# Seven products instead of eight for the values and gates of two retention heads in a four-layer decoder trunk

## Chip, cores and metric

One core of a Trainium2 chip. The metric is the device time of one execution in microseconds, the median of several runs. All numbers are in fp32; a matmul operand is split into two fp32r parts, so that a product takes three matmuls.

## What is computed

Four layers on 256 tokens with 1024 features. The mixer of layer i is number i mod 3: retention in layers 0 and 3, dilated attention in layer 1, a gated MLP in layer 2. Each is followed by a SwiGLU channel mixer and a gated embedding of the layer. The change is about retention's values v and gates g:

```python
proj = h @ w_in
q, k, v, g = jnp.split(proj, [H * dk, 2 * H * dk, 2 * H * dk + H * dv], axis=-1)   # H=4, dk=256, dv=512
...
scores = jnp.einsum('bnhk,bmhk->bhnm', qc, kc) * decay_mask[None]
inner = jnp.einsum('bhnm,bmhv->bnhv', scores, vc)
...
y = y * lax.rsqrt(jnp.mean(y * y, axis=-1, keepdims=True) + EPS)
return (jax.nn.silu(g) * y) @ w_out
```

## The kernel before

All work is issued in the order in which the Python code runs (`tc.manual_schedule`); each engine takes its own instructions strictly in that order. PE is TensorE, DVE is VectorE, ACT is ScalarE, SP issues all loads.

**Weights.** Every weight is streamed once, as a list of entries per layer (`_plan`), 128 x 1024 values each, two entries to a load of 1 MB into a ring of four `raw` buffers. `split_one` (line 197) makes of an entry a chunk that a matmul can read: ACT copies it to `wh` (line 204), DVE takes the rest to `wl` (line 208). `USES` lists the chunks in the order in which they are used; one entry can be used several times, and a use can first add another entry to it in place (line 207, an add on DVE). Splits are pumped ahead: each `Chunk(...)` in the code takes the next chunk and lets one more be split, at most `LEAD = 6` beyond the one taken. `pump(n)` and the table `P` place further splits at fixed points.

**Products.** `token_major` (line 367) multiplies 256 tokens with 512 columns: four chunks of 12 matmuls of 512 columns, 48 in all. `feature_major` (line 335) makes 256 columns for q, k and the like: two chunks of 24 matmuls of 256 columns. Results lie in the PSUM pool "ps" with four banks; `acc`, in four other banks, collects the output projection, `row` adds one row block of `w_out` (12 matmuls of 512 columns).

**Retention** (line 477) goes over four heads `hd`. For each: v by `token_major`, evacuated by `ev_v` (ACT to `vh`, DVE to `vl`); then `t_of(z)`, the transposes of the head before; q and k by `feature_major` and their rotation on DVE (`ta`, `tb`, `qkl`) and ACT (`qkh`); g by `token_major` (`ev_g`, ACT to `sg`), with the scores (`sc`, `sh`, `sl`) before its last chunk; two rows of `w_out` for the head before; the two products `ys`; their norm (squares `junk` and square root on ACT, reciprocal on DVE) and `z`; two more rows.

**The channel mixer** (line 962) already has two blocks, `seven(i)`, in which gate and up of 512 columns are made by seven half-size products (Strassen's scheme in Winograd's form) instead of eight: p1, p5, p6, p1 again with more, p7, p3, p4, each of two chunks with six matmuls of 512 columns. Its left operands are blocks of `a_hi`, `a_lo` and four sums of such blocks, `s0` to `s3`, which `make_sums` prepares once per layer: 13 operations of 512 columns on DVE (9 sums and 4 rests) and 4 copies on ACT. The right ones are weights added in place: a unit of 8 entries gives 14 chunks with 8 adds. The results are put together on DVE in `u2`, `u4` and `up1`. There p4 is added to p7 in p7's own bank, which DVE must have read before (line 1099, `hid`).

Of the kernel before, what the change touches and what calls it, by code (L numbers as in the profile page):

```python
# [31 lines left out]
    rate=1, s0=2, s1=1, i0=2, i1=1, ar0=0, ar1=0, ar2=1, a0=0, a1=1,  # L32
# [21 lines left out]
def _plan(l):  # L54
    kind, j = l % 3, l // 3
    emb = _rows("ple_w_proj", l, 0, 2)
    mix = []
    if kind == 0:
        for h in range(4):
            mix += _cols("ret_w_in", j, 2048 + 512 * h, 512, 2)  # L60
            mix += _blocks("ret_w_in", j, 256 * h, 2) + _blocks("ret_w_in", j, 1024 + 256 * h, 2)
            mix += _cols("ret_w_in", j, 4096 + 512 * h, 512, 2)
            if h:
                mix += _rows("ret_w_out", j, 4 * h - 4, 2)
                mix += emb if h == 3 else []
                mix += _rows("ret_w_out", j, 4 * h - 2, 2)
        mix += _rows("ret_w_out", j, 12, 4)
    elif kind == 1:
        for p in range(8):
            cols = tuple((g * 3072 + 2048 + 128 * p, 128) for g in range(3))  # L70
            mix += [("attn_w_in", j, 2 * c, 2, cols) for c in range(4)]
            for g in range(3):
                for w in range(2):
                    mix += _blocks("attn_w_in", j, g * 3072 + w * 1024 + 128 * p, 1)
        mix += emb + _rows("attn_w_out", j, 0, 8)
    else:
        for c0 in (2048, 2560, 3072, 3584, 0, 512, 1024):
            mix += _cols("gm_w_in", j, c0, 512, 2)
        mix += _rows("gm_w_out", j, 0, 4) + _cols("gm_w_in", j, 1536, 512, 2)
        mix += _rows("gm_w_out", j, 4, 6) + emb + _rows("gm_w_out", j, 10, 6)  # L80
    mix += _cols("ffn_w_in", l, 0, 512, 2) + _cols("ffn_w_in", l, HID, 512, 2)
    uses = [(e, None) for e in range(len(mix))]

    def plain(ds):
        uses.extend((len(mix) + i, None) for i in range(len(ds)))
        mix.extend(ds)

    for i, seven in UNITS:
        if seven:
# [1224 lines left out]
```

## Time and profile before

| | |
|---|---|
| runs | 1703.89, 1704.80, 1705.27 us; median 1704.8 us |
| profiled execution | 1703.74 us, span 1702.0 us (1.7 us lie around the span) |
| PE busy | 1685.1 us (99%), 9867 matmuls |
| DVE busy | 1309.8 us (77%), 1851 instructions |
| ACT busy | 1037.9 us (61%), 1578 instructions |
| loaded | 311 MB, 184 GB/s over the span |

Busy time is the union of an engine's rows. A matmul's row goes from its start to the modelled end of its results, and the next one starts before that; the distance of starts is its pace. "Idle before" and the waits name what an engine waited for last.

### The profile page before, as it was taken

The numbers are of one execution on the slowest core, as the hardware profiler recorded it, in microseconds if no ns is written. First come the engines' busy times: TensorE is split into PE (matmuls) and PEld (weight loads), VectorE is DVE, ScalarE is ACT, GpSimd is POOL, SyncE is SP. The second block draws the span as 40 slices with busy tenths as digits, with TensorE's granted clock in tenths as the row PEclk, the third lists the DMA queues.
The fourth block names the chain that finished last, engine by engine and source line by source line (L and its number), as shares of the span: only waits on it lengthen the run. The fifth ranks groups of instructions, "written<-read, shape, count | busy, mean of one in ns | idle before, by whom it ended". The sixth has DMA issues, their size and how long they took to land.

```text
span 1702.0 us, 24880 instructions
## 1 busy us (share of the span) xinstructions
PE 1685.1 (99%) x9867; PEld 1492.8 (88%) x9867; DVE 1309.8 (77%) x1851; ACT 1037.9 (61%) x1578; POOL 0.2 (0%) x4
## 2 busy tenths in 40 slices
PE   9999999999999999999999999999999999999998
PEld 7888889888999999889888888898888888889887
DVE  7666578897888888778987675778977665678986
ACT  6555665557776767655567654745567555665555
POOL 0000000000000000000000000000000000000000
PEclk9999999999999999999999999999999999999999
DMA  8644453664655555453564744554464554553560
GB/s 291 227 154 178 170 210 124 223 223 151 200 178 166 170 171 178 124 207 124 223 247 149 280 178 151 191 206 177 173 221 167 192 183 173 176 208 124 223 241 31
DMA packets 53588, 314.14 MB, mean 185 GB/s; under 512 B 5632, under 2 KB 13616, under 8 KB 19168
## 3 DMA queue, kind: packets, MB, share of 16 engines
q1 hardware_dynamic: 53472, 312.56, 51.4%
q8 instruction: 77, 1.26, 0.3%
q14 instruction: 39, 0.32, 0.1%
HBM read 311.41 MB, written 1.12 MB: 184 GB/s over the span
## 4 chain that ended last, share of the span: by engine, by line
PE 84%; DVE 8%; ACT 4%; DMA 2%; issue 2%; ACTq 0%; SPq 0%; DVEq 0%
PE ps L237 18%; PE ps L239 18%; PE ps L238 18%; PE acc L237 7%; PE acc L239 7%; PE acc L238 7%; DVE wl L208 4%; ACT wh L204 2%; PE ps L357 2%; PE ps L358 2%; PE ps L361 2%; DMA raw<-in_w_dram 2%; DVE raw L207 1%; PE acc L295 1%; PE ps L286 1%
## 5 line engine op out<-in xcount | busy, mean ns | idle before, releaser
L208 DVE TENSOR_TENSOR wl<-raw,wh 128x1024 fp32r<-128x1024 f32 x615 | 715.0, 1206 | 85.4 <-ACT wh L204 82.0
L204 ACT ACTIVATE wh<-raw 128x1024 fp32r<-128x1024 f32 x615 | 608.4, 1040 | 117.0 <-DMA raw<-in_w_dram 44.0
L237 PE MATMUL ps<-a_hi,wh 128*128 128x256 f32 x1280 | 365.6, 286 | 0.0
L239 PE MATMUL ps<-a_hi,wl 128*128 128x256 f32 x1280 | 362.5, 283 | 0.0
L238 PE MATMUL ps<-a_lo,wh 128*128 128x256 f32 x1280 | 362.5, 283 | 0.0
L237 PE MATMUL ps<-wh,a_hi 128*128 128x512 f32 (+2 forms) x728 | 278.8, 383 | 7.5 <-DVE hid L1099 6.0
L238 PE MATMUL ps<-wl,a_hi 128*128 128x512 f32 (+2 forms) x728 | 276.2, 379 | 0.0
L239 PE MATMUL ps<-wh,a_lo 128*128 128x512 f32 (+2 forms) x728 | 276.1, 379 | 0.1
L238 PEld LDWEIGHTS ps<-a_lo,wh 128*128 128x128 f32 x1280 | 245.8, 192 | 0.9
L237 PEld LDWEIGHTS ps<-a_hi,wh 128*128 128x128 f32 x1280 | 245.7, 192 | 0.9
L239 PEld LDWEIGHTS ps<-a_hi,wl 128*128 128x128 f32 x1280 | 245.7, 192 | 0.0
L237 PEld LDWEIGHTS ps<-wh,a_hi 128*128 128x128 f32 x728 | 137.2, 188 | 34.8 <-ACT wh L204 9.1
L239 PEld LDWEIGHTS ps<-wh,a_lo 128*128 128x128 f32 x728 | 137.0, 188 | 24.3 <-DVE a_lo L300 0.9
L238 PEld LDWEIGHTS ps<-wl,a_hi 128*128 128x128 f32 x728 | 137.1, 188 | 23.2 <-DVE wl L208 0.8
L297 ACT ACTIVATE a_hi<-acc,gc 128x128 fp32r<-128x128 f32 x192 | 52.2, 382 | 43.6 <-PE acc L295 43.4
L207 DVE TENSOR_TENSOR raw<-raw 128x1024 f32<-128x1024 f32 x64 | 78.1, 1221 | 0.8
L237 PE MATMUL acc<-wh,h 128*128 128x512 f32 x192 | 75.0, 390 | 0.0
L238 PE MATMUL acc<-wl,h 128*128 128x512 f32 x192 | 74.9, 390 | 0.0
L239 PE MATMUL acc<-wh,h 128*128 128x512 f32 x192 | 74.8, 389 | 0.0
L237 PE MATMUL acc<-wh,hh 128*128 128x512 f32 x160 | 62.7, 392 | 0.0
L238 PE MATMUL acc<-wl,hh 128*128 128x512 f32 x160 | 62.4, 390 | 0.0
L239 PE MATMUL acc<-wh,hl 128*128 128x512 f32 x160 | 62.3, 389 | 0.0
(258 smaller groups left out, 2472.7 us busy)
## 6 DMA issues: line engine op xcount, KB each, us to landing
raw<-in_w_dram SPq DMA_DIRECT2D x266, 1024.0 KB, 5.0
raw<-in_w_dram SPq DMA_DIRECT2D x16, 768.0 KB, 4.5
gain<-in_norm_g_dram SPq DMA_DIRECT2D x8, 512.0 KB, 6.2
bias<-vec SPq DMA_DIRECT2D x8, 384.0 KB, 7.3
emb<-vec SPq DMA_DIRECT2D x8, 384.0 KB, 8.9
ln<-in_gm_ln_dram SPq DMA_DIRECT2D x2, 1024.0 KB, 7.5
raw<-in_w_dram SPq DMA_DIRECT2D x3, 512.0 KB, 8.3
dec<-in_c_decay_dram SPq DMA_DIRECT2D x4, 384.0 KB, 5.5
```

Of the source, the lines that this page charges most:

```text
L204: act.activation(out=hi[:, 0:n], in_=raw, func=AF.Copy)
L207: dve.tensor_tensor(out=entry(c + 1), in0=entry(c + 1), in1=entry(c + 1, 3), op=ALU.add)
L208: dve.tensor_tensor(out=lo[:, 0:n], in0=raw, in1=hi[:, 0:n].bitcast(F32), op=ALU.subtract)
L237: pe.matmul(ps, lhsT=lh, rhs=rh, start=start, stop=False, skip_group_check=more)
L238: pe.matmul(ps, lhsT=lh, rhs=rl, start=False, stop=False, skip_group_check=more)
L239: pe.matmul(ps, lhsT=ll, rhs=rh, start=False, stop=stop, skip_group_check=more)
L286: pe.transpose(ps[:, cut(i, 128)], src[:, cut(i, 128)], ident)
L295: pe.transpose(ps[:, cut(i, 128)], src[:, cut(i, 128)], ident)
L297: act.activation(out=dst_hi[:, k0 + i, tok(tt)], in_=ps[:, cut(i, 128)], func=AF.Copy, scale=gain(k0 + i))
L357: pe.matmul(ps, lhsT=a, rhs=w.hi[:, k, :], start=kk == 0, stop=False)
L358: pe.matmul(ps, lhsT=a, rhs=w.lo[:, k, :], start=False, stop=False)
L361: pe.matmul(ps, lhsT=a_lo[:, kk, tok(tt)], rhs=w.hi[:, k, :], start=False, stop=kk == 7)
```

## The change

In heads 1 and 3 of both retention layers (`SEVEN_HEADS`), v and g, 512 columns each, are made together by seven products like gate and up of the channel mixer, ahead of q and k. The code for it is taken out of `ffn` and shared: `make_sums` and `product_of_seven`. The sums of layer input blocks are made at the end of head 0. The transposes `t_of(z)` move between p3 and p4. `ev_seven` takes v and g of both token halves; g comes with its sign turned and gets a negative scale (`minus_r`). Since g is no longer made after k, the scores follow the first row of `w_out`. In `product_of_seven` p4 has a bank of its own, and `u2` gets p7 by one more sum on DVE; that holds for the channel mixer too. The vectors of the relative bias (`rel_vectors`), prepared in layer 0's retention in heads 1 to 3, are prepared in layer 0's channel mixer, in units 2 to 4. At the end of layer 0 two splits fewer are pumped before the second half of attention's input is transposed (rate 0 instead of 2 for `g2`, one later instead of none), and `i0` is 1 instead of 2. The scratch for dynamic DMAs is set to 1024.

```diff
-    rate=1, s0=2, s1=1, i0=2, i1=1, ar0=0, ar1=0, ar2=1, a0=0, a1=1,
+    rate=1, s0=2, s1=1, i0=1, i1=1, ar0=0, ar1=0, ar2=1, a0=0, a1=1,
...
+    def seven(name, j, c0, c1):
+        e = len(mix)
+        a, b = _cols(name, j, c0, 512, 2), _cols(name, j, c1, 512, 2)
+        mix.extend(b[0:2] + a[0:2] + b[2:4] + a[2:4])
+        for at, add in ((2, None), (2, 0), (2, 4), (6, None), (0, 4), (4, None), (6, 2)):
+            uses.extend((e + at + c, None if add is None else e + add + c) for c in range(2))
...
+            if h in SEVEN_HEADS:
+                seven("ret_w_in", j, 2048 + 512 * h, 4096 + 512 * h)
+            else:
+                plain(_cols("ret_w_in", j, 2048 + 512 * h, 512, 2))
...
+SEVEN_HEADS = (1, 3)
...
+    def make_sums(pool, temps):
+        t21, t11, s1 = temps
...
+        def split(n, t):
+            parts = [pool.tile([128, 4, 128], F32R, name=f"s{n}{p}") for p in "hl"]
+            act.activation(out=parts[0], in_=k4(t), func=AF.Copy)
+            dve.tensor_tensor(out=parts[1], in0=k4(t), in1=parts[0].bitcast(F32), op=ALU.subtract)
+            return parts
...
+    def product_of_seven(name, sums, temps, evac, middle):
+        def prod(a, ps=None):
+            more = ps is not None
+            ps = ps if more else ps_tile()
+            for c in range(2):
+                w = Chunk(name)
+                for k in range(2):
+                    kk = 2 * c + k
+                    mm3(ps, a[0][:, kk, :], a[1][:, kk, :], w.hi[:, k, :], w.lo[:, k, :], not more and kk == 0,
+                        kk == 3, more)
+                w.release()
+            return ps
+        u2, u4, up = temps
+        p1 = prod(block(0, 0))
+        act.activation(out=u2, in_=p1, func=AF.Copy)
+        p5 = prod(sums[0])
+        p6 = prod(sums[1])
+        dve.tensor_tensor(out=u2, in0=p6, in1=u2, op=ALU.add)
+        dve.tensor_tensor(out=u4, in0=p5, in1=u2, op=ALU.add)
+        prod(block(0, 1), p1)
+        evac(0, 0, p1)
+        p7 = prod(sums[2])
+        dve.tensor_tensor(out=up, in0=p7, in1=u4, op=ALU.add)
+        dve.tensor_tensor(out=u2, in0=p7, in1=u2, op=ALU.add)
+        p3 = prod(sums[3])
+        dve.tensor_tensor(out=u4, in0=p3, in1=u4, op=ALU.add)
+        evac(0, 1, u4)
+        middle()
+        p4 = prod(block(1, 1))
+        dve.tensor_tensor(out=u2, in0=p4, in1=u2, op=ALU.add)
+        evac(1, 0, u2)
+        evac(1, 1, up)
...
+            def ev_seven(tt, second, src):
+                if second:
+                    act.activation(out=sg[:, tt, :], in_=src, func=AF.Silu, scale=minus_r[tt])
+                else:
+                    ev_v(tt, src)
+
+            if hd in SEVEN_HEADS:
+                turned_z = []
+                product_of_seven(name, sums, sevens(), ev_seven, lambda: turned_z.append(t_of(z)))
+            elif hd:
                 token_major(name, ev_v)
...
-            if l == 0 and hd == 1:
-                rel_part = rel_vectors(mp)
-            if l == 0 and hd > 1:
-                rel_part[hd - 2]()
-            token_major(name, ev_g, before={3: scores})
+            if hd not in SEVEN_HEADS:
+                token_major(name, ev_g, before={3: scores})
+            if hd == 0 and SEVEN_HEADS:
+                sums = make_sums(mp, sevens())
...
                     row(w, zz, k, acc, hd == 1 and k == 0, False)
                     w.release()
+                    if k == 0 and hd in SEVEN_HEADS:
+                        scores()
...
-            prod(p7, block(1, 1), False, True)
-            dve.tensor_tensor(out=u2, in0=p7, in1=u2, op=ALU.add)
...
+            product_of_seven(name, sums, flats(), evac, lambda: rows(i - 1, ks=(0,)))
...
         pump(P["g1"])
-        st["rate"] = P["g2"]
+        to_attention = (l + 1) % 3 == 1
+        st["rate"] = 0 if to_attention else P["g2"]
...
-            pump(P["g4"])
+            pump(1 if to_attention else P["g4"])
...
-    nc = _bacc.Bacc("TRN2", target_bir_lowering=False, num_devices=1)
+    nc = _bacc.Bacc("TRN2", target_bir_lowering=False, num_devices=1, dynamic_dma_scratch_size=1024)
```

What this makes of the order shows at three places. (In rows of the changed kernel, lines are those of its own file: 215 is the add of raw weights, 216 the split on DVE, 245 to 247 the three matmuls of a product.)

DVE at the end of head 0 in layer 0, from the scores on. Before:

```order
27 L546 TENSOR_TENSOR sc<-ps,dec 128x384
28 L548 TENSOR_TENSOR sl<-sc,sh 128x384
29 L208 TENSOR_TENSOR wl<-raw,wh 128x1024
30 L272 RECIPROCAL sm<-sm 128x2
31 L582 SCALAR_TENSOR_TENSOR z<-ps,sm,sg 128x512 x2
32 L208 TENSOR_TENSOR wl<-raw,wh 128x1024 x4
33 L498 SCALAR_TENSOR_TENSOR vl<-ps,sm,vh 128x512 x2
```

Now, from the last of the sums on:

```order
47 L440 TENSOR_TENSOR pn<-pn,st 128x512
48 L422 TENSOR_TENSOR s3l<-pn,s3h 128x512
49 L657 TENSOR_SCALAR minus_572<-sm 128x1
50 L657 TENSOR_SCALAR minus_574<-sm 128x1
51 L280 RECIPROCAL sm<-sm 128x2
52 L687 SCALAR_TENSOR_TENSOR z<-ps,sm,sg 128x512 x2
53 L216 TENSOR_TENSOR wl<-raw,wh 128x1024 x2
54 L215 TENSOR_TENSOR raw<-raw 128x1024
55 L216 TENSOR_TENSOR wl<-raw,wh 128x1024
56 L215 TENSOR_TENSOR raw<-raw 128x1024
57 L216 TENSOR_TENSOR wl<-raw,wh 128x1024 x3
58 L463 TENSOR_TENSOR st<-ps,st 128x512
```

The 13 operations of the sums stand between the scores and `z`, and behind `z` begin the splits of head 1's block with their adds (rows 54 and 56).

PE at the beginning of head 1 in layer 0, with buffer numbers and waits. Before, the first product of the values:

```order
242 L239 MATMUL ps_544<-vh_166,sl_450 128x512
243 L237 MATMUL ps_544<-vh_166,sh_449 128x512
244 L238 MATMUL ps_544<-vl_167,sh_449 128x512
245 L239 MATMUL ps_544<-vh_166,sl_450 128x512
246 L237 MATMUL ps_569<-wh_408,a_hi_83 128x512 [waits Activation_49]
247 L238 MATMUL ps_569<-wl_409,a_hi_83 128x512
248 L239 MATMUL ps_569<-wh_408,a_lo_84 128x512
```

Now, the end of p5 and the product p6 (`ps_651`):

```order
267 L245 MATMUL ps_628<-wh_487,s0h_546 128x512
268 L246 MATMUL ps_628<-wl_488,s0h_546 128x512
269 L247 MATMUL ps_628<-wh_487,s0l_547 128x512
270 L245 MATMUL ps_651<-wh_520,s1h_553 128x512 [waits DVE_49,Activation_49]
271 L246 MATMUL ps_651<-wl_521,s1h_553 128x512
272 L247 MATMUL ps_651<-wh_520,s1l_554 128x512
273 L245 MATMUL ps_651<-wh_520,s1h_553 128x512
274 L246 MATMUL ps_651<-wl_521,s1h_553 128x512
275 L247 MATMUL ps_651<-wh_520,s1l_554 128x512
276 L245 MATMUL ps_651<-wh_607,s1h_553 128x512 [waits Activation_49]
277 L246 MATMUL ps_651<-wl_608,s1h_553 128x512 [waits DVE_49]
278 L247 MATMUL ps_651<-wh_607,s1l_554 128x512
```

The first matmul of p6 waits for DVE, though the first half of its weights was split long before: its bank is one that `z` has to read. The first matmuls of its second chunk wait for that chunk's split.

DVE in head 1 of layer 0 from the splits ahead of k's rotation to the reading of the scores (`sc`). Before:

```order
41 L208 TENSOR_TENSOR wl<-raw,wh 128x1024 x2
42 L521 TENSOR_TENSOR ta<-ps,turned 128x512
43 L522 TENSOR_TENSOR tb<-ps,turned 128x512
44 L523 TENSOR_TENSOR ta<-ta,tb 128x256
45 L524 TENSOR_TENSOR ta<-ta,tb 128x256
46 L528 TENSOR_TENSOR qkl<-ta,qkh 128x512
47 L208 TENSOR_TENSOR wl<-raw,wh 128x1024 x3
48 L546 TENSOR_TENSOR sc<-ps,dec 128x384
49 L548 TENSOR_TENSOR sl<-sc,sh 128x384
50 L208 TENSOR_TENSOR wl<-raw,wh 128x1024 x3
```

Now:

```order
80 L216 TENSOR_TENSOR wl<-raw,wh 128x1024 x2
81 L626 TENSOR_TENSOR ta<-ps,turned 128x512
82 L627 TENSOR_TENSOR tb<-ps,turned 128x512
83 L628 TENSOR_TENSOR ta<-ta,tb 128x256
84 L629 TENSOR_TENSOR ta<-ta,tb 128x256
85 L633 TENSOR_TENSOR qkl<-ta,qkh 128x512
86 L216 TENSOR_TENSOR wl<-raw,wh 128x1024
87 L646 TENSOR_TENSOR sc<-ps,dec 128x384
88 L648 TENSOR_TENSOR sl<-sc,sh 128x384
89 L216 TENSOR_TENSOR wl<-raw,wh 128x1024
```

One split lies between k's rotation and the scores instead of three, since a row of `w_out` has taken the place of three chunks of g.

## Rows read from the trace of the kernel before

**Rows 1.** The page: busy time of PE, and PE's granted clock by slice.

```profile
PE 1685.1 (99%) x9867; PEld 1492.8 (88%) x9867; DVE 1309.8 (77%) x1851; ACT 1037.9 (61%) x1578; POOL 0.2 (0%) x4
...
PEclk9999999999999999999999999999999999999999
```

**Rows 2.** Windows: us; busy us (count) of PE, PEld, DVE, ACT, POOL; clock; DMA.

```profile
48.00:58.92 10.92, 10.92 (x49) 9.05 (x49) 6.44 (x8) 7.97 (x12) 0.00 (x0) 1.00 0.34 129
59.82:71.38 11.56, 11.56 (x99) 11.56 (x98) 8.80 (x12) 5.51 (x8) 0.00 (x0) 1.00 0.39 137
```

**Rows 3.** Waits of PE: line, releaser, us in total, times, longest.

```profile
PE ps L237 <- DVE hid L1099: 6.0, 8, 1.1
PE ps L1219 <- DVE warm L1214: 1.5, 1, 1.5
PE ps L357 <- ACT a_hi L297: 1.2, 1, 1.2
PE ps L237 <- DVE band L956: 0.9, 1, 0.9
PE ps L237 <- DVE tb L522: 0.6, 1, 0.6
```

**Rows 4.** Timeline of DVE, layer 0, head 0's end: start, us, operation, count.

```profile
39.53 0.69 DVE L528 TENSOR_TENSOR qkl<-ta,qkh 128x512 fp32r<-128x512 f32 x1 [0.70 <-ACT qkh L527]
40.48 3.50 DVE L208 TENSOR_TENSOR wl<-raw,wh 128x1024 fp32r<-128x1024 f32 x3 [0.26 <-ACT wh L204]
43.89 0.55 DVE L546 TENSOR_TENSOR sc<-ps,dec 128x384 f32<-128x384 f32 x1
45.03 0.56 DVE L548 TENSOR_TENSOR sl<-sc,sh 128x384 fp32r<-128x384 f32 x1 [0.59 <-ACT sh L547]
...
51.61 0.17 DVE L272 RECIPROCAL sm<-sm 128x2 f32<-128x2 f32 x1 [4.40 <-ACT sm L270]
51.81 1.41 DVE L582 SCALAR_TENSOR_TENSOR z<-ps,sm,sg 128x512 f32<-128x512 f32 x2
```

**Rows 5.** Timeline of DVE in a block of seven products, layer 0's mixer.

```profile
286.88 1.22 DVE L207 TENSOR_TENSOR raw<-raw 128x1024 f32<-128x1024 f32 x1
...
289.27 1.23 DVE L207 TENSOR_TENSOR raw<-raw 128x1024 f32<-128x1024 f32 x1
...
304.75 0.68 DVE L1090 TENSOR_TENSOR gr<-ps,gr 128x512 f32<-128x512 f32 x1
...
308.93 1.22 DVE L208 TENSOR_TENSOR wl<-raw,wh 128x1024 fp32r<-128x1024 f32 x1 [1.64 <-ACT wh L204]
...
314.76 0.68 DVE L1099 TENSOR_TENSOR hid<-ps,gr 128x512 f32<-128x512 f32 x1
```

**Rows 6.** Timeline of DVE: first and last of 13 sum operations, layer 0's mixer.

```profile
252.92 0.68 DVE L1042 TENSOR_TENSOR gr<-a_hi,a_lo 128x512 f32<-128x512 f32 x1
...
263.79 0.69 DVE L1047 TENSOR_TENSOR s3l<-pn,s3h 128x512 fp32r<-128x512 f32 x1 [0.70 <-ACT s3h L1046]
```

**Rows 7.** Timeline of ACT, layer 0, head 0's end.

```profile
48.55 1.28 ACT L555 ACT_TABLE_LOAD   x1
49.84 0.60 ACT L266 ACTIVATE junk<-ps 128x512 bf16<-128x512 f32 x1
```

**Rows 8.** Timeline of PE: first matmul of y, head 0, layers 0 and 3.

```profile
45.80 0.39 PE L237 MATMUL ps<-vh,sh 128*128 128x512 f32 x1
...
1324.47 0.39 PE L237 MATMUL ps<-vh,sh 128*128 128x512 f32 x1
```

**Rows 9.** Timeline of DVE, head 1, layer 0: k's rotation, first and last.

```profile
71.88 0.68 DVE L521 TENSOR_TENSOR ta<-ps,turned 128x512 f32<-128x512 f32 x1
...
74.66 0.69 DVE L528 TENSOR_TENSOR qkl<-ta,qkh 128x512 fp32r<-128x512 f32 x1 [0.70 <-ACT qkh L527]
```

**Rows 10.** Timeline of DVE, layer 3, head 0: end of k's rotation.

```profile
1316.55 0.69 DVE L528 TENSOR_TENSOR qkl<-ta,qkh 128x512 fp32r<-128x512 f32 x1 [0.70 <-ACT qkh L527]
```

**Rows 11.** Timeline of PE: first matmul of p1, layer 0's mixer.

```profile
295.52 0.39 PE L237 MATMUL ps<-wh,a_hi 128*128 128x512 f32 x1
```

More of the change, by code (lines that the diff above doesn't have):

```diff
@@ L389, in token_major, with block, k4, pn @@
             evac(tt, ps[tt])
+    def block(tt, half):
+        return [t[:, 4 * half:4 * half + 4, tok(tt)] for t in (a_hi, a_lo)]
+    def make_sums(pool, temps):
+        t21, t11, s1 = temps
+        def k4(t):
+            return t.rearrange("p (k t) -> p k t", k=4)
+        def pn():
+            return tmp_p.tile([128, 512], F32, tag="pn", name="pn")
+        def whole(t, tt, half):
+            hi, lo = block(tt, half)
+            dve.tensor_tensor(out=k4(t), in0=hi.bitcast(F32), in1=lo.bitcast(F32), op=ALU.add)
+            return t
+        def split(n, t):
[3 more added lines that the diff above has]
+            return parts
+        sums = []
+        whole(t21, 1, 0)
+        t22 = whole(pn(), 1, 1)
+        dve.tensor_tensor(out=s1, in0=t22, in1=t21, op=ALU.subtract)
+        sums.append(split(0, s1))
+        whole(t11, 0, 0)
+        s2 = pn()
+        dve.scalar_tensor_tensor(out=s2, in0=s1, scalar=-1.0, in1=t11, op0=ALU.mult, op1=ALU.subtract)
+        sums.append(split(1, s2))
+        s3 = pn()
+        dve.tensor_tensor(out=s3, in0=t11, in1=t21, op=ALU.subtract)
+        sums.append(split(2, s3))
+        t12 = whole(pn(), 0, 1)
+        dve.tensor_tensor(out=t12, in0=t11, in1=t12, op=ALU.subtract)
+        s4 = pn()
+        dve.tensor_tensor(out=s4, in0=t12, in1=s1, op=ALU.add)
+        sums.append(split(3, s4))
+        return sums
@@ L490, in t_of, with sevens @@
             return zz
+        def sevens():
+            return [mp.tile([128, 512], F32, tag="st", name="st", bufs=3) for _ in range(3)]
         for hd in range(4):
@@ L509, in retention @@
             else:
[L510 removed]
+                zz = turned_z[0] if hd in SEVEN_HEADS else t_of(z)
             qk = []
@@ L934, in rel_vectors @@
     def rel_vectors(rp):
-        room = emb.rearrange("p a b -> p (a b)")[0:32, :]
-        hot, rel = room[:, 0:1152].rearrange("p (g u) -> p g u", g=3), room[:, 1152:1200]
+        rel = rp.tile([32, 48], F32, name="rel")
+        hot = rp.tile([32, 3, 384], F32, name="hot")
         band = rp.tile([16, 3, 384], F32, name="band")
@@ L1029, in rows @@
                     c.release()
-        sums = [[fp.tile([128, 4, 128], F32R, name=f"s{n}{p}") for p in "hl"] for n in range(4)]
-        def block(tt, half):
-            return [t[:, 4 * half:4 * half + 4, tok(tt)] for t in (a_hi, a_lo)]
-        def k4(t):
-            return t.rearrange("p (k t) -> p k t", k=4)
-        def whole(t, tt, half):
-            hi, lo = block(tt, half)
-            dve.tensor_tensor(out=k4(t), in0=hi.bitcast(F32), in1=lo.bitcast(F32), op=ALU.add)
-            return t
@@ new lines, in flats, with evac @@
+        def flats():
+            return [flat("gr"), flat("gr"), flat("hid")]
+        def seven(i):
+            s = [fp.tile([128, 512], F32, tag="s0", name="s0", bufs=2) for _ in range(2)]
+            def evac(tt, second, src):
+                if second:
+                    dve.scalar_tensor_tensor(out=hid0[tt], in0=src, scalar=-1.0, in1=s[tt], op0=ALU.mult, op1=ALU.mult)
+                else:
+                    act.activation(out=s[tt], in_=src, func=AF.Silu, scale=r[tt])
+            product_of_seven(name, sums, flats(), evac, lambda: rows(i - 1, ks=(0,)))
@@ L1124, in ffn @@
                 gain = load_gain(l, 3)
+                if l == 0:
+                    rel_part = rel_vectors(fp)
+            if l == 0 and i in (3, 4):
+                rel_part[i - 3]()
             up = feature_major(name)
@@ L1127, in ffn @@
             if i == 2:
-                make_sums()
+                sums = make_sums(fp, flats())
             rows(i - 2, i == NPAIR - 1)
```

113 lines of the change are left out of this document (28 added, 85 removed).

## Prediction

> **What bounds the kernel now.** I read the page first, then the waits of TensorE, then stretches of the timelines. The page says that TensorE is busy for 99% of the span, and at 9 tenths or more of full clock in each of the 40 slices [rows 1]. That share alone misleads, because a matmul's row lasts longer than the time to the next start. So I took the pace from stretches: 48 matmuls of 512 columns fill 10.92 us, 0.228 us each, and 96 of 256 columns fill 11.56 us, 0.120 us each [rows 2] (each window also counts a matmul or more that began before it). TensorE's waits are tiny: eight of 6.0 us in sum, one of 1.5 at the start, and single ones of 1.2, 0.9 and 0.6 us [rows 3]. TensorE therefore runs from start to end with hardly a hole. A matmul that goes saves its full pace, and each new wait is added in full to the end. The question is only whether the work that the change puts on VectorE (DVE) stays under TensorE's work.
>
> Prices on DVE: a split is 1.15 us (three take 3.50, the last of them 1.2 [rows 4]), an add of raw weights with the split behind it 2.39 us (from one add's start at 286.88 to the next at 289.27 [rows 5]), an operation on 512 columns 0.65 us (0.68 with its end [rows 5]).
>
> **What the change takes away.** In each of heads 1 and 3 of both retention layers, 96 matmuls for values and gates become 84. Four heads times 12 times 0.228 us: **-10.9 us**. In the dense channel mixer the fourth product gets a bank of its own, so the eight waits for `hid` go: **-6.0 us** [rows 3]. The added `u2` sum of 0.65 us on DVE is covered there: until TensorE needs what follows, it has a row and a feature-major product to do, over 8 us. At attention's opening two splits leave ScalarE's queue ahead of `a_hi`: **-1.2 us** [rows 3]; the later ones lie beside q and k products. I keep 0 to -4 as bounds, since pair 0's and pair 1's splits move too. The bias vectors' work moves out of head 3 of layer 0, where it cost waits of 0.9 and 0.6 us: **-1.5 us** [rows 3]. Its six small matmuls stay, now among units whose blocks take 2.9 us of TensorE per split of 1.15. Its three loads and one store on SP's queue move with it; the loads behind the store serve splits that come later on DVE too, so I cost that at nothing (at most, one wait for raw weights of 1.6 us, as in the mixer's unit [rows 5]). The smaller scratch for dynamic DMAs only makes room in SBUF, and I cost it at nothing: nothing in the order is issued from that engine. Together **-19.6 us**.
>
> **Opening of head 1, layer 0.** DVE is done with k's rotation at 40.22 (39.53 + 0.69 [rows 4]). Now three add-and-split pairs stand there instead of three splits: 7.2 us, to 47.4. The scores' chain `sc`, `sh`, `sl` lasts 1.7 us: it begins as the three splits end (43.89) and ends at 45.59 [rows 4]. Now it ends at 49.1. One more pair: 51.5. Then come the sums. In the channel mixer they took from 252.92 to 263.79, where `s3h` is done and the last split starts, 10.8 us with a round trip to ScalarE for each sum [rows 6]: 62.3 here. ScalarE's queue holds a table load (1.28) and the sums of squares behind `s3h`; from the first of these to DVE's reciprocal are 1.77 us, and 0.9 more to the end of the first `z` [rows 4, 7]. So `z` of the first half comes at **66.3**, of the second at 67.0.
>
> What waits for it: the pool "ps" has four banks. The two `y`, p1 and p5 hold them, so p6 needs a bank of `y`, and that comes back when `z` has read it. Before, a whole product of 48 matmuls [rows 2] lay between, and the next tile to need that bank was the transpose of `z` itself. TensorE ends the gates at 45.80 [rows 8]; `y` (9 matmuls), p1 and p5 (24) take 7.5 us, to 53.3. Hole: **13.0 us**.
>
> **The rest of that head.** DVE starts with no lead. Until it has read p7 for the second time it has 4 pairs, 6 splits and 5 operations of 512 columns: 9.6 + 6.9 + 3.3 = 19.8, from 67.0 to 86.8. p4 needs p7's bank (p3 and the two transposes hold the other three). TensorE, from 66.3, needs four products of 2.73 and 0.9 for transposes, to 78.1. Hole: 8.7. q needs p3's bank, which DVE reads two splits later: 0.2. After q and k (11.6 us) TensorE is at 101.3.
>
> Then the scores. The gates' last part used to lie between k and them, now only one row of `w_out` does (12 matmuls, 2.7 us, to 104.0). DVE still has two transposes' splits, four weight splits and two sums to do before q's rotation, at 97.0; with that (3.5 us, [rows 9]) and two splits k's begins at 103.0, 2.8 us before kh and 3.5 before kl can be used [rows 9]: holes of 1.8 and 0.5. If DVE were on time, 0.9 would be left, the lower bound. Sum for this head: 13.0 + 8.9 + 2.3 = **+24.2 us**.
>
> **Head 1, layer 3.** One pair fewer stands ahead of the scores. From 1317.24 [rows 10]: 6.2 to 1323.4, scores 1325.1 (TensorE asks for `sl` at 1324.92), a pair 1327.5, then 10.8 + 1.28 + 1.77 + 0.9: `z` at 1342.3 and 1343.0, and p6's first weights one pair later, 1345.4. TensorE would be ready at 1324.47 + 7.5 = 1332.0 [rows 8]: 13.4. Then 5 pairs, 5 splits and 5 small operations: 21.0, to 1364.0, against 1357.2: 6.8. With 0.2 and 2.3: **+22.7 us**.
>
> **Heads 3.** No sums are made here, and two rows of `w_out` on either side of `y` give DVE time. But p1 starts when DVE has only the fourth of fourteen splits ready, since `p_lo`, `z` and four adds lie ahead of it. By the same addition `u2` is done with p7 22.7 us after p1's start, and TensorE is there after 17.3 us (six products, transposes): 5.4. The channel mixer shows the nearest row: `hid`, read from p7, ended at 315.44, 19.9 us after p1's start at 295.52 [rows 5, 11], with a full lead; with the second read 20.6, which leaves 3.3, the lower bound. I take 5.0, nearer the addition, because the order has that work ahead of p1. With 2.3 for the scores: **+7.3 us** each, 14.6 for both.
>
> **Sum.** 24.2 + 22.7 + 14.6 = 61.5 of holes, less 19.6: +41.9. The profiled execution took 1703.7 us (span 1702.0), 1.1 below the median of the runs; 1703.7 + 41.9 + 1.1 = 1746.7, forecast **1746 us**. Its own range is 1732 to 1756: down to it reach 3.3 and 0.9 for the smaller holes (4 x 1.4 + 2 x 1.7 = 9 us) and 5 us for attention's opening and for pairs that come closer together; up, a wait for raw weights in each of the four blocks, of which the mixer's unit shows one of 1.64 us [rows 5], and nothing gained at attention's opening.
>
> **Rivals.** (1) *Faster, 1685 us.* DVE's lag stays covered, and only the -19.6 remain. For it: the mixer's units do the same arithmetic, and there TensorE waits only for `hid`. Place and point: the first `z` would have to come at 53.3 in layer 0, so the sums would have to begin 13 us earlier on DVE, before k's rotation, or DVE would have to be idle there. Against: it works without a pause from 40.5 to the scores even now [rows 4]. Chance 0.08.
> (2) *Only the openings cost, about 1716 us.* DVE catches up by p4, so that 13.0 + 13.4 and four times 0.9 remain: +30.0 - 19.6 = +10.4. It would take DVE operations that overlap more than the rows do; the mixer's lag of 19.9 speaks against it. Chance 0.13.
> (3) *The clock, about 1758 us.* The trace shows full clock everywhere [rows 1], and after the start no pause of TensorE longer than 1.2 us [rows 3], so no row tells what a hole of 9 to 13 us does. In my sum a slower p6 and p1' would cost nothing, because DVE sets p4's start. If half of q's product after p4 ran at half rate, 24 matmuls would cost 0.120 us more each, 2.9 us in each of four heads: +11.6. The Trainium skill, in "TensorE: Matmul & The Clock Gate", section "HAM oscillation — how this bites in real kernels", says that idle gaps of the engine send its clock back to half rate and that the work after each starts slow; no run here shows it yet, and it would give the 1758. Chance 0.08.
> (4) The change is there and moves nothing that can be measured: holes and savings cancel within 3.4 us. About 0.2% is what a measurement of this kernel can tell from no change. Chance 0.03.
>
> **Numbers.** Main case 0.68, (2) 0.13, (3) 0.08, (1) 0.08, (4) 0.03. The range 1714 to 1756 holds the main case and (2) and leaves out (1), (3) and most of (4), 0.19. Faster 0.08, same 0.03, slower 0.89.
>
> **What would show it.** The waits of TensorE must list `ps` on `z` of DVE, once in each retention layer, near 10 us; `ps` on DVE's `st` in all four heads, 3 to 9 us; and `qkh`/`qkl` at the scores. DVE's busy time must rise by about 100 us (per head 6 splits and 8 adds at 1.15 and six small sums; twice 13 operations of sums; 8 for the mixer), TensorE's must fall by some 11 while its idle time grows by 50 to 60. I am wrong if p6 finds its bank free, that is, if the gap between p5 and p6 in layer 0 is under 5 us, or if p4 starts within 18 us of p1.

## The result, and the profile after

The changed kernel takes 1766.7 us (median of four runs, 1765.0 to 1769.0), the kernel before 1704.4: a ratio of 1.0366, interval 1.0350 to 1.0381. The forecast was 1746, its range ended at 1756. The sign was right and so was the kind of cause, but 20.7 us are missing from the sum. The profiled execution has a span of 1763.3 us where that of before had 1702.0.

The page of the changed kernel, busy time of the engines and PE's granted clock by slice, against [rows 1]:

```profile
PE 1697.2 (96%) x9819; PEld 1494.0 (85%) x9819; DVE 1410.4 (80%) x1969; ACT 1069.5 (61%) x1614; POOL 0.2 (0%) x4
...
PEclk9899899999999999999999999999999899999999
```

TensorE runs 48 matmuls fewer, as forecast, and yet its busy time has grown by 12 us, where the prediction had it fall by 11; its idle time has grown by 49 (50 to 60 were forecast). VectorE's (DVE) busy time has grown by 100.6, as forecast. Why TensorE's has grown shows in the second row: three slices (44 to 88, 176 to 220 and 1367 to 1411 us) no longer stand at 9 tenths of full clock. All three lie in the retention layers.

The waits of PE (line, releaser, us in total, times, longest), against [rows 3]:

```profile
PE ps L245 <- DVE z L687: 17.9, 2, 9.0
PE ps L245 <- DVE st L469: 12.2, 4, 3.2
PE ps L245 <- ACT qkh L632: 11.4, 4, 4.4
PE ps L246 <- DVE wl L216: 5.9, 7, 2.1
PE ps L245 <- ACT sh L647: 2.2, 1, 2.2
...
PE ps L788 <- ACT th L777: 1.6, 1, 1.6
...
PE ps L245 <- DVE band L1060: 0.8, 1, 0.8
```

The first three waits are the three forecast ones: `z` twice, once in each retention layer; `st` in all four heads; `qkh` at the four scores. Two more are new: `wl`, of which 3.3 us stand behind the wait for `z` in layer 3, and `sh`, on which `y` of head 0 in layer 0 waits. The eight waits for `hid` ahead of the fourth product and the one for `a_hi` at attention's opening are gone. The wait for `band` is still there, in the mixer now, and one for `th` (1.6 us) stands in attention's first pair, where before had none as long.

The opening of head 1 in layer 0, first on DVE, then on PE (start, us, line, operation, in brackets the idle time before it and what ended it):

```profile
55.76 0.69 DVE L422 TENSOR_TENSOR s1l<-pn,s1h 128x512 fp32r<-128x512 f32 x1 [0.70 <-ACT s1h L421]
...
57.74 0.69 DVE L422 TENSOR_TENSOR s2l<-pn,s2h 128x512 fp32r<-128x512 f32 x1 [0.69 <-ACT s2h L421]
...
61.19 0.69 DVE L422 TENSOR_TENSOR s3l<-pn,s3h 128x512 fp32r<-128x512 f32 x1 [0.69 <-ACT s3h L421]
...
64.23 0.17 DVE L280 RECIPROCAL sm<-sm 128x2 f32<-128x2 f32 x1 [2.23 <-ACT sm L278]
64.44 1.41 DVE L687 SCALAR_TENSOR_TENSOR z<-ps,sm,sg 128x512 f32<-128x512 f32 x2
```

```profile
55.99 0.40 PE L247 MATMUL ps<-wh,s0l 128*128 128x512 f32 x1
65.33 0.76 PE L245 MATMUL ps<-wh,s1h 128*128 128x512 f32 x1 [8.95 <-DVE z L687]
```

DVE works through the sums, with a pause of 0.7 us for ScalarE (ACT) at each, before it comes to `z`, as in [rows 6]. p5 ends, p6 waits for a bank of `y`, and it starts as the first `z` has been read: at 65.3 us, where the forecast had 66.3.

Windows of PE: that hole, the 5.1 us behind it, and the time around the later hole ahead of p4 in head 3 (columns: window, its length, busy us and count, granted clock, DMA share, GB/s):

```profile
55.99:65.33 9.34, 0.39 (x2) 0.72 0.00 0
65.33:70.47 5.14, 5.14 (x12) 0.51 0.00 0
...
190.20:197.00 6.80, 5.37 (x14) 0.53 0.89 326
```

In the hole the granted clock falls, and p6's 12 matmuls run at 0.51, the lower of the clock's two levels (1.2 GHz): 5.1 us instead of the 2.73 of a product at full clock. A fall of the clock is what rival (3) rested on, which the forecast had given a chance of 0.08. The Trainium skill says in "TensorE: Matmul & The Clock Gate", section "HAM oscillation — how this bites in real kernels", that the clock goes back to half rate in such idle gaps, and the trace agrees (0.72 in the hole, 0.51 behind it). What it costs here is another matter, and the experiments answer it.

Where p4, the scores and `y` start, against the forecast. For layer 3 the forecast's times are moved by the 28.9 us by which the program is later at the end of head 0's gates. "Scores to y" was 4.7 us in the forecast: 4.2 by the pace of 24 matmuls (12 of 256 and 12 of 512 columns), and the hole of 0.5 for the rest of k, which lies behind the first scores.

| | forecast | measured |
|---|---|---|
| head 1, layer 0: p6 / p4 | 66.3 / 86.8 | 65.3 / 85.2 |
| head 1, layer 3: p6 / p4 | 1374.3 / 1392.9 | 1371.2 (its second matmul 1374.0) / 1392.6 |
| heads 3: p1 to p4 | 22.3 | 21.7 and 23.1 |
| p4 to the scores, all four heads | 19.0 | 21.82 in each |
| scores to y, all four heads | 4.7 | 6.4, 6.1, 6.3, 4.8 |

The openings and p4 came where they were forecast, to 2 us or better. What failed stands in the last two rows: 11.3 us too little between p4 and the scores, 4.8 behind them. The number that stays at 21.82, in four heads with different holes ahead of p4 and different clocks, is the clue that the experiments follow.

### The profile page after: what moved, and what is told of

Read it like the earlier page. It is cut to its first block, busy times and chain, and to the rows that moved or that the text cites. A ratio compares the mean times of both kernels' runs of the same rounds, so it can differ in the third digit from the quotient of the medians.

```text
span 1763.3 us, 24972 instructions
## 1 busy us (share of the span) xinstructions
PE 1697.2 (96%) x9819; PEld 1494.0 (85%) x9819; DVE 1410.4 (80%) x1969; ACT 1069.5 (61%) x1614; POOL 0.2 (0%) x4
## 4 chain that ended last, share of the span: by engine, by line
PE 69%; DVE 17%; ACT 7%; issue 4%; DMA 2%; ACTq 0%; SPq 0%; DVEq 0%
PE ps L247 14%; PE ps L245 14%; PE ps L246 14%; DVE wl L216 8%; PE acc L245 6%; PE acc L246 6%; PE acc L247 6%; ACT wh L212 3%; DMA raw<-in_w_dram 2%; DVE raw L215 2%; PE ps L365 2%; PE ps L366 2%; PE ps L369 2%; PE acc L303 1%; PE ps L294 1%
## 5 line engine op out<-in xcount | busy, mean ns | idle before, releaser
L216 DVE TENSOR_TENSOR wl<-raw,wh 128x1024 fp32r<-128x1024 f32 x639 | 746.2, 1207 | 79.0 <-ACT wh L212 75.9
L212 ACT ACTIVATE wh<-raw 128x1024 fp32r<-128x1024 f32 x639 | 633.8, 1041 | 165.3 <-DVE raw L215 80.9
L245 PE MATMUL ps<-wh,a_hi 128*128 128x512 f32 (+2 forms) x648 | 249.6, 385 | 14.0 <-DVE st L469 12.2
L246 PE MATMUL ps<-wl,a_hi 128*128 128x512 f32 (+2 forms) x648 | 247.3, 382 | 0.2 <-DVE wl L199 0.2
L247 PE MATMUL ps<-wh,a_lo 128*128 128x512 f32 (+2 forms) x648 | 247.1, 381 | 0.0
L245 PEld LDWEIGHTS ps<-wh,a_hi 128*128 128x128 f32 x648 | 123.4, 190 | 35.8 <-ACT wh L212 13.0
L247 PEld LDWEIGHTS ps<-wh,a_lo 128*128 128x128 f32 x648 | 123.3, 190 | 21.6 <-DVE a_lo L308 0.8
L246 PEld LDWEIGHTS ps<-wl,a_hi 128*128 128x128 f32 x648 | 123.5, 191 | 20.8 <-DVE wl L199 0.5
L215 DVE TENSOR_TENSOR raw<-raw 128x1024 f32<-128x1024 f32 x96 | 117.2, 1220 | 1.1
```

The costliest lines, as they stand in the source:

```text
L212: act.activation(out=hi[:, 0:n], in_=raw, func=AF.Copy)
L215: dve.tensor_tensor(out=entry(c + 1), in0=entry(c + 1), in1=entry(c + 1, 3), op=ALU.add)
L216: dve.tensor_tensor(out=lo[:, 0:n], in0=raw, in1=hi[:, 0:n].bitcast(F32), op=ALU.subtract)
L245: pe.matmul(ps, lhsT=lh, rhs=rh, start=start, stop=False, skip_group_check=more)
L246: pe.matmul(ps, lhsT=lh, rhs=rl, start=False, stop=False, skip_group_check=more)
L247: pe.matmul(ps, lhsT=ll, rhs=rh, start=False, stop=stop, skip_group_check=more)
```

## The experiments

Twelve kernels ran. They are told by question and not in the order in which they ran; times are medians, ratios are to the kernel before on the same chip.

**1. No seven products in the heads.** How much of the result lies outside the retention heads?

```
-SEVEN_HEADS = (1, 3)
+SEVEN_HEADS = ()
```

> The retention heads go back to plain products; p4's own bank in the mixer, attention's opening and the moved bias vectors stay. By the prediction's terms (-6.0, -1.2, -1.5) it should take 1695.6 us. By the offsets between the two traces at matching matmuls (mixer blocks -5.0 us in sum; attention's opening -1.4 that pair 0 gives back; the vectors' wait moved, not removed) it should take 1699 us. A rival by which a good part of the +62 us lies outside the retention heads wants 1704 or more.

Measured: 1699.4 us, ratio 0.9971 (0.9961 to 0.9982). The retention heads carry the whole loss and more: 67 us. What is outside them gains 5.0, as the offsets between the traces said, not the 8.7 of the prediction's terms.

**2 and 3. The two small parts alone.** The first is the kernel of experiment 1 with attention's opening as before (`i0`, the rate and the pumps), so that it keeps p4's bank and the vectors' new place. The second is the kernel before with p4's bank and nothing else:

```
             dve.tensor_tensor(out=up1, in0=p7, in1=u4, op=ALU.add)
+            dve.tensor_tensor(out=u2, in0=p7, in1=u2, op=ALU.add)
...
-            prod(p7, block(1, 1), False, True)
-            dve.tensor_tensor(out=u2, in0=p7, in1=u2, op=ALU.add)
+            p4 = ps_tile()
+            prod(p4, block(1, 1))
+            dve.tensor_tensor(out=u2, in0=p4, in1=u2, op=ALU.add)
```

> No seven products in the heads, and attention's opening as before: what stays is p4's own bank in the mixer and the bias vectors' new place. With all three parts it took 1699.4 us; the offsets of that trace put about -5 us on the mixer's blocks, -1 on the vectors and +0.6 to +1.2 on attention's opening, whose wait only moves to pair 0. If so, 1698 to 1699. By the prediction's terms the opening was worth -1.2: 1700.6.

> The kernel before with one edit: the fourth product of the mixer's blocks in a bank of its own. By the prediction's term -6.0: 1698.3; by the mixer's offsets in the trace of the change, -5.0: 1699.3. If the waits for hid were replaced by others behind it, 1702 or more.

Measured: 1697.7 us (ratio 0.9958, 0.9945 to 0.9972) and 1699.2 (0.9970, 0.9959 to 0.9981). p4's bank brings 5.3 us. The vectors' move brings another 1.5 and attention's opening costs 1.7, both by medians alone: the intervals of the ratios overlap. The trace tells why the opening brings nothing: the kernel without it has `a_hi` back, and a wait for `th` of only 0.3 us. (The rate for `g2` in the kernel before is 1, not 2 as the section on the change has it.)

```profile
PE ps L365 <- ACT a_hi L305: 1.2, 1, 1.2
```

The kernel of the first of these two runs is the fastest of the study by its median, and it beats the kernel before as well as the change.

**4. The sums behind z.** Is it the bank of `y` that costs, or the amount of DVE's work?

```
-            if hd == 0 and SEVEN_HEADS:
-                sums = make_sums(mp, sevens())
...
                 dve.scalar_tensor_tensor(out=z[:, tt, :], in0=ys[tt], scalar=ry[:, tt:tt + 1], in1=sg[:, tt, :],
                                          op0=ALU.mult, op1=ALU.mult)
+            if hd == 0 and SEVEN_HEADS:
+                sums = make_sums(mp, sevens())
...
```

> The sums are made after z of head 0, so that y's banks come back early. If VectorE's amount of work sets the pace, p6 no longer waits on z, but p5 on s0 and the weights behind it instead, p4 in layer 0 starts within 2 us of 85 us, and the time stays within 4 us of 1766.7. If the bank was the cost, the holes of 9.1 and 11.7 us go: about 1747.

Measured: 1769.2 us, ratio 1.0381 (1.0365 to 1.0396). The wait on `z` is gone, and these are in its place:

```profile
PE ps L245 <- DVE st L469: 12.2, 4, 3.2
...
PE ps L245 <- ACT s0h L421: 9.0, 2, 4.8
PE ps L245 <- ACT wh L212: 6.1, 2, 4.0
```

p4 starts at 87.5, 2.3 us later than before, and the time is the same but for 2.5 us. The bank is only the place where the wait shows. DVE's work sets p4, whichever of the sums and `z` comes first.

**5. The sums left out.**

```
-                sums = make_sums(mp, sevens())
+                sums = [block(1, 0), block(0, 0), block(1, 1), block(0, 1)]
```

> The change with one thing left out in the retention layers: the sums are not made, and the products take blocks of a_hi and a_lo in their place (so values and gates of heads 1 and 3 come out otherwise). If the sums are what delays z, p6 waits only for the adds ahead of z: z comes 10.8 us earlier, p6 in layer 0 near 57 instead of 65.3, and the time is about 20 us lower, 1745 to 1749 (the kernel with head 3 alone showed +10.4 in each layer from the sums).

Measured: 1745.9 us, ratio 1.0239 (1.0224 to 1.0254): 20.8 us less than the change, 10.4 a layer. p6 in layer 0 starts at 56.9, as expected. No wait on `z` is left, but the other two stand as they were:

```profile
PE ps L245 <- DVE st L469: 12.2, 4, 3.2
PE ps L245 <- ACT qkh L632: 11.8, 4, 3.0
```

**6. Seven products in head 3 alone.** What do the sums cost where head 1 is plain?

```
-SEVEN_HEADS = (1, 3)
+SEVEN_HEADS = (3,)
```

> Seven products in head 3 alone; the sums are still made at the end of head 0. By the offsets between the traces head 1 of layer 0 costs 24.9 us net of its saving and that of layer 3 24.6: without them 1766.7 - 49.5 = 1717. If the sums in front of z cost by themselves, also where head 1 is plain (its transposes of z come 48 products after the gates, 11 us), 1 to 5 us more in each layer: 1719 to 1727.

Measured: 1738.6 us, ratio 1.0203 (1.0187 to 1.0218), 11.6 us above the upper expectation. I had thought that a plain head 1, whose transposes of `z` come 11 us after the gates, would hide most of the sums. It does not: by the matmuls' offsets to the kernel before, head 1 loses 9.9 us in layer 0 and 10.4 in layer 3 from `y` of head 0 to the scores. Most of it lies in these waits (for `z` itself and for the bank that `vl` reads):

```profile
PE ps L245 <- DVE vl L589: 8.4, 2, 4.5
...
PE ps L294 <- DVE z L687: 5.4, 2, 2.9
```

When q's product starts, 8.1 and 7.8 us of it are there; the sums take 10.8, so that some 3 are hidden. The other 1.8 and 2.7 us come behind, because the first matmuls of q run at the lower clock:

```profile
58.00:64.00 6.00, 3.12 (x15) 0.84 0.00 0
64.00:70.00 6.00, 2.12 (x10) 0.50 0.76 295
```

(These are windows of PE in layer 0, with the columns as above.) DVE has little slack at the end of head 0: most of what is put there comes out at the end, wherever TensorE asks next.

**7. The raw adds left out.**

```
-        if c + 1 < len(chunks) and chunks[c + 1][3] is not None:
+        if c + 1 < len(chunks) and chunks[c + 1][3] is not None and chunks[c + 1][0][0] != "ret_w_in":
```

> The 32 adds of raw weights in the retention heads are left out, so that values and gates there are computed from other weights; every other instruction stays. VectorE has 8 x 1.15 = 9.2 us less in each of the four heads. If its queue sets p6 and p4, z in heads 1 comes 3 to 4 adds earlier (4 us) and p4 another 4 to 5, and in heads 3 the holes ahead of p4 (4.3 us and 4.2) go: 8 to 9 and 4 to 6 us per head, 1738 to 1743. If the holes are of round trips and banks alone, 1760 or more.

Measured: 1743.6 us, ratio 1.0226 (1.0208 to 1.0245): 23.0 us less than the change, and 0.6 above the range expected. The holes ahead of p4 go. p6 comes 2.7 us earlier in layer 0 (62.7), but p5 ends 2.1 earlier too, so that the wait for `z` hardly shrinks, and the scores wait longer:

```profile
PE ps L245 <- ACT qkh L632: 17.6, 4, 4.4
PE ps L245 <- DVE z L687: 16.5, 2, 8.4
...
PE ps L245 <- DVE st L469: 1.1, 1, 1.1
```

From p4 to the scores are 21.82, 21.71, 21.79 and 21.70 us here. DVE comes to p4 with 9.2 us less work behind it, and that distance hardly moves. In both kernels DVE's queue has the same instructions from the second read of p7, just ahead of p4, to the scores, no add among them, and it pauses there for ScalarE alone. Work ahead of p4 moves this chain, and does not change its length.

**8. The adds on GpSimd.** Would the idle engine take them?

```
-            dve.tensor_tensor(out=entry(c + 1), in0=entry(c + 1), in1=entry(c + 1, 3), op=ALU.add)
+            adder = nc.gpsimd if chunks[c + 1][0][0] == "ret_w_in" else dve
+            adder.tensor_tensor(out=entry(c + 1), in0=entry(c + 1), in1=entry(c + 1, 3), op=ALU.add)
```

> The 32 adds of raw weights of the retention heads (1.22 us each on VectorE) go to GpSimd, which is idle. If VectorE's queue sets the holes, each head has 8 x 1.2 = 9.8 us less of it: the waits on st and at the scores in heads 3 go (about 12 us with the clock), z in heads 1 comes 4 to 5 us earlier and p4's hole goes: about 1735. If GpSimd's add lasts over 3 us, or VectorE's operations stretch beside it, the weights wait for it and the time is 1767 or more.

Measured: 1792.9 us, ratio 1.0517 (1.0500 to 1.0535). The trace by line (durations in ns, least, median, greatest) shows both halves of the second alternative:

```profile
L216 DVE TENSOR_TENSOR raw<-raw x64: 1215/1220/1226, 327.1 to 1725.2; 128x1024 f32<-128x1024 f32 x64
L216 POOL TENSOR_TENSOR raw<-raw x32: 2358/3256/3447, 37.3 to 1515.1; 128x1024 f32<-128x1024 f32 x32
...
L217 DVE TENSOR_TENSOR wl<-raw,wh x639: 942/1219/3424, 11.7 to 1770.9; 128x1024 fp32r<-128x1024 f32 x152, 128x768 fp32r<-128x768 f32 x8
```

The same add lasts 3.26 us there against 1.22 on DVE, and a split of DVE, which never lasts over 1.23 us in the change, lasts up to 3.42 beside it. All 18 splits that last over 1.3 us overlap with an add of GpSimd. TensorE's waits for `wl` rise from 5.9 to 16.1 us. The Trainium skill, in "SBUF — State Buffer", section "Who interferes with whom", says that an operation of VectorE with two inputs in SBUF and one of GpSimd that reads SBUF shut each other out of a port that they share; the splits of 3.42 us agree.

**9 and 10. The clock.** Products of zeros keep TensorE at work in the holes. In the first trial those behind p5 went to p1's bank. In the second, shown here, all go to one bank of the pool "acc", which in heads 1 is still free and in heads 3 has zeros added to it.

```
+    def fill(ps, n, first=False):
+        for i in range(n):
+            pe.matmul(ps, lhsT=zero[:, 0:128], rhs=zero, start=first and i == 0, stop=i == n - 1,
+                      skip_group_check=True)
...
         p5 = prod(sums[0])
+        if fills and fills[0]:
+            fill(fills[2], fills[0], True)
...
         middle()
+        if fills:
+            fill(fills[2], fills[1], fills[3])
         p4 = prod(block(1, 1))
...
                     if k == 0 and hd in SEVEN_HEADS:
+                        fill(acc[0][0], 14)
                         scores()
```

> Zeros are multiplied on TensorE where it waited: 38 products of 512 columns after p5 in heads 1 (8.6 us in holes of 9.1 and more), 12 ahead of p4 and 9 ahead of the scores in heads 1 and 3. They add nothing to any sum. If the half clock after the holes is what the prediction left out, the periods at 0.5 that follow p6, p4 and the scores go, and with them most of their 12 us: 1755 to 1759. If VectorE alone sets p4 and the scores (the prediction's main case, where a slow p6 costs nothing), the time stays within 2 us of 1766.7. If the fillers last longer than the holes, it gets slower.

> Products of zeros again, now in a bank of the pool acc for all of them, so that they wait for no copy of ScalarE: 38 after p5 in heads 1 (8.6 us), 14 ahead of p4 and 14 ahead of the scores in heads 1 and 3 (3.2 us each). The periods at half clock after p6, p4 and the scores should go. If VectorE and ScalarE set p4 and the scores whatever TensorE's clock, only what runs at half rate behind the scores comes back, 1.5 + 1.1 + 1.3 + 0.2 = 4.2 us by the trace of the change: about 1762.5. If all matmuls at half rate lie on the path, 12 us: about 1755.

Measured: 1774.3 us (ratio 1.0411, 1.0395 to 1.0426) and 1764.8 (1.0356, 1.0341 to 1.0371). The first says nothing on the clock. Its products had to wait until ScalarE had copied p1, which stands behind the sums in ScalarE's queue, so that they ran behind the hole and not in it:

```profile
PE ps L447 <- ACT st L465: 22.5, 2, 12.2
```

In the second they do what they should nearly everywhere. In layer 0 the window of the hole and the one behind it are at full clock, where the change had 0.72 and 0.51, and the mean granted clock rises from 0.986 to 0.997; in layer 3 p6 is still slow (0.62 over its 7.7 us):

```profile
56.30:66.66 10.36, 9.58 (x45) 1.00 0.00 0
66.66:69.30 2.64, 2.64 (x11) 1.00 0.00 0
```

And the time is only 1.9 us lower, with intervals that overlap. In layer 0 p6 starts 19.8 us ahead of p4 with and without the full clock, and in all four heads p4 starts 21.8 ahead of the scores. Only from the scores to `y` does the full clock give something back: 4.8 us in all four heads instead of 6.4, 6.1, 6.3 and 4.8, 4.3 us in sum. The windows from the scores to `y` in head 1 of layer 0, first in the change, then here:

```profile
106.96:113.31 6.35, 6.13 (x24) 0.73 0.76 280
```

```profile
108.29:113.11 4.82, 4.59 (x24) 1.00 0.77 275
```

The spans of the two profiled executions differ by 0.9 us only, since 3.5 of the 4.3 are lost again elsewhere: 1.3 before head 1's first product in layer 0, as much in layer 2's mixer, the rest in smaller parts. The prediction's main case said that a slow p6 costs nothing because DVE sets p4. That holds.

**11. Gates and values evaluated later.** The chain from p4 to the scores, in head 3 of layer 0, on DVE of the changed kernel:

```profile
190.81 0.68 DVE L469 TENSOR_TENSOR st<-ps,st 128x512 f32<-128x512 f32 x1
191.41 2.35 DVE L216 TENSOR_TENSOR wl<-raw,wh 128x1024 fp32r<-128x1024 f32 x2
193.67 0.68 DVE L471 TENSOR_TENSOR st<-ps,st 128x512 f32<-128x512 f32 x1
195.63 1.29 DVE L298 TENSOR_TENSOR zz<-ps,zz 128x512 fp32r<-128x512 f32 x2 [1.27 <-ACT zz L297]
...
200.82 0.75 DVE L589 SCALAR_TENSOR_TENSOR vl<-st,sm,vh 128x512 fp32r<-128x512 f32 x1 [0.79 <-ACT vh L588]
202.38 2.36 DVE L216 TENSOR_TENSOR wl<-raw,wh 128x1024 fp32r<-128x1024 f32 x2 [0.81 <-ACT wh L212]
204.65 0.68 DVE L626 TENSOR_TENSOR ta<-ps,turned 128x512 f32<-128x512 f32 x1
...
207.43 0.69 DVE L633 TENSOR_TENSOR qkl<-ta,qkh 128x512 fp32r<-128x512 f32 x1 [0.70 <-ACT qkh L632]
...
213.43 0.69 DVE L633 TENSOR_TENSOR qkl<-ta,qkh 128x512 fp32r<-128x512 f32 x1 [0.69 <-ACT qkh L632]
```

DVE and ACT pass the work to and fro. DVE's `st` at 193.67 has to be done before ACT can evaluate the gate (from 194.39), and only behind that gate in ACT's queue stand the copies of the transposes, on which DVE's `zz` waits. Between the end of the second read of p7 (L469, 191.5), for which p4 waits, and the scores (213.4) DVE waits for ACT for 4.5 us in all and is busy for the rest, some 17.4. The three pauses ahead of q's rotation (1.27, 0.79 and 0.81) make 2.9 of it. The edit moves the evaluations and nothing else:

```
-        evac(0, 1, u4)
         middle()
+        evac(0, 1, u4)
...
-        evac(1, 0, u2)
-        evac(1, 1, up)
+        rest.append(lambda: evac(1, 0, u2))
+        rest.append(lambda: evac(1, 1, up))
...
             (qh, ql), (kh, kl) = qk
+            if hd in SEVEN_HEADS:
+                for f in rest:
+                    f()
```

> ScalarE copies the transposes of z before it evaluates the gate of the first half, and the values and gates of the second half are evaluated behind k's rotation instead of behind p4. No work is added or removed. Between p4's start and the scores VectorE idles 1.3, 0.8 and 0.8 us for ScalarE there, and 0.75 us of its work moves behind. If these round trips are what the prediction's counting of busy time left out (21.8 us from p4 to the scores in all four heads, where it had 19.5), the scores come 2 to 3.6 us earlier in each head: 1753 to 1759. If VectorE's busy time alone counts, 1765 to 1769.

Measured: 1754.9 us, ratio 1.0299 (1.0284 to 1.0315): 11.7 us less than the change, without an instruction removed. From p4 to the scores are now 19.2, 20.3, 19.2 and 18.4 us instead of 21.8. The waits at the scores shrink to 1.8 us, and a new one appears behind them, of `y` for `sh` (2.3 of its five waits is head 0's, the four others about 0.9 each):

```profile
PE ps L245 <- DVE z L699: 17.3, 2, 9.0
...
PE ps L245 <- ACT sh L659: 5.9, 5, 2.3
...
PE ps L245 <- ACT qkh L641: 1.8, 4, 1.0
```

**12. Much of DVE's added work out.** Experiments 5, 7 and 11 in one kernel. Of the 95.6 us of busy time that the change has on DVE over the kernel of experiment 1, 39.5 stay, mostly the six more splits and the small sums of each head.

> Neither the sums nor the adds of raw weights in the retention layers, and the values and gates of the second half evaluated behind k's rotation: most of what the change put on VectorE is left out, the 84 products a head stay. If VectorE's work and the round trips through ScalarE are the whole cause, p6, p4 and the scores hardly wait and the saved products count: 1699.4 - 10.9 = 1688.5 at the least, and up to 1698 with holes of 1 to 2 us left at the scores and at p4. If something else holds TensorE (banks, clock), it stays above 1704.

Measured: 1705.4 us, ratio 1.0006 (0.9997 to 1.0016). My expectation missed. It is 17 us above 1688.5: the saved 10.9 us are spent, with the adds of raw weights and the sums at the opening gone and the clock at 0.999:

```profile
PE ps L245 <- ACT qkh L641: 3.9, 4, 1.0
PE ps L245 <- ACT sh L659: 3.6, 4, 0.9
PE ps L245 <- DVE st L469: 3.3, 2, 2.4
```

p4 to the scores takes 18.3 to 18.4 us in all four heads, where TensorE's own work there (p4, q, k and a row of `w_out`) is 17.0; the scores to `y` take 5.9, where it is 4.2. That makes 3 us in each head, 12 in all, and the waits for `st` another 3.3. DVE's queue still sets the scores: in head 1 of layer 0 its trace has no pause from p6's sums to k's rotation other than 2.2 us for ScalarE. Two causes stand here that no run separates. One is the work that is left on DVE. The other is cover that the change took away: before, the gates' 48 products lay between k and `y`: in head 1 q's start to the scores took 19.8 us and the scores to `y` 9.6, with no wait in either. Now one row of `w_out` lies ahead of the scores and one behind them. A kernel with more rows moved there was not tried, so that the share of each cause stays open.

## Why the prediction was wrong, point by point

**What held.** TensorE bounds the kernel, each new wait is added in full, and DVE's work sets the waits: experiments 4, 5, 7 and 12 show it. The wait of p6 for `z` is there, in the two places forecast, at 65.3 against 66.3 us. In layer 0 it lasts 8.9 and not 13.0 us, as TensorE comes to it 2.9 us late: the prediction let `y` of head 0 start at 45.8 though it had moved `sl` to 49.1, and `y` waits 2.2 us for `sh` there. That moves the hole and not its end. The price of the sums, 10.8 us from [rows 6], came out as 10.4 a layer in experiment 5. p4 came 1.6 us early in head 1 of layer 0, within 0.3 us in layer 3, and within 0.8 in the heads 3. DVE's busy time grew by 100.6 us, as forecast. Rivals (1), (2) and (4) fell: the first two wanted the lag to be covered or caught up, the last wanted it to be made good by the savings.

**The step that failed first: "holes of 1.8 and 0.5" at the scores.** The prediction counted DVE's busy time from p4 on (six weight splits, two of them named with q's bank, two transposes' splits, two sums, a rest of v) to q's rotation, and came to 19.0 us to the scores. Between these it left out the trips to ScalarE, though it had priced such trips for the sums and within the rotations. The trace has three of them there, 2.9 us in sum, and 21.8 us to the scores in all four heads: 4 x 2.8 = 11.3 us. Experiment 7 shows that less work ahead of p4 does not shorten the stretch, experiment 11 that another order of the trips does.

**The second: the lower clock was priced at nothing behind the scores.** The prediction's 4.7 us from the scores to `y` came out as 6.4, 6.1, 6.3 and 4.8, 4.8 us too little in four heads. At full clock all four take 4.8 (experiment 10), so that 4.3 us are matmuls at the lower level: there TensorE has next to nothing to wait for, and a slow matmul counts. The prediction also overlooked that the gates had lain between the scores and `y`. In the change that costs no wait; in experiments 11 and 12, where the scores come earlier, `y` waits 0.9 us for `sh` in each head, and the stretch takes 5.9.

**The clock.** Rival (3) saw rightly that the clock would fall in the holes, and its price of 11.6 us was wrong: it let q's product after p4 count. There DVE and ScalarE set the scores, and p6, p4 and q run slowly in time that they would have waited anyway. Where it does cost, behind the scores, the rival did not look. Experiment 10 gives 1.9 us for the full clock nearly everywhere, by medians whose intervals overlap, and 4.3 by the stretches from the scores to `y`.

**The credits were too large.** The prediction had -6.0 for p4's bank, -1.2 for attention's opening and -1.5 for the vectors, -8.7 in sum; all three together gave -5.0 (experiment 1). The bank alone gave 5.3. At the opening the wait only changed its place: `a_hi` 1.2 us went, `th` 1.6 us came (0.3 before), although the prediction had named the pairs' moved splits as the open end of that term. The saved products' -10.9 is right as work, since 48 matmuls went, but experiment 12 shows it all spent again with more than half of DVE's added work out.

**The ledger.** 11.3 and 4.8 us at and behind the scores, less 1.7 by which p4 came early, and 3.7 of credit too much: 18.1 us. The spans of the two traces lie 61.3 us apart where 41.9 were forecast, so 19.4 are to be found. Of the rest 0.7 lies in heads 2, from `y` to `y`, and 0.6 is not placed. (The forecast of 1746 was itself 0.7 under its sum of 1746.7.)

## What to carry to other kernels

When work is put on an engine that is 77% busy, price its chain at the place and not its share: write down in order what that engine does and add each trip to another engine and back, since its pauses for the other engine lengthen the chain as its work does. Then ask of each product that is moved or dropped what it was covering, both ahead of it and behind it; here the products for values and gates had been the cover of q's, k's and the scores' chains, and without them nothing was left of the saving even with more than half of DVE's added work taken out. A distance that stays the same while the work ahead of it changes has its cause within it; here a change of order there shortened it.

## What the hardware showed that was not expected

TensorE's granted clock fell to the lower level not only in the holes of 9 us but also around pauses of 3 us: it stood at 0.53 in the window from 190.2 to 197.0 us of the change, which holds the end of such a pause ahead of p4 and the product after it. Behind pauses of about 2 us ahead of the scores it stood at 0.72 and 0.73 up to `y` in layer 0. Zeros multiplied in the pauses held it at 1.00 in these places. And of some 90 matmuls at half the clock most cost nothing, because TensorE would have waited for another engine in that time; those behind the scores cost 4.3 us.

GpSimd, idle in both kernels, is no free adder: an add that takes VectorE 1.22 us took it 3.26, splits of VectorE lasted up to 3.42 us beside it, and the kernel was 26 us slower than the change.
